# Expert layer of a two-layer trunk: two of eight experts go from 64 places to 32, and the turns are set anew

## The chip, the cores and the metric

The kernel runs on one core of a Trainium2 chip. The metric is the device time of one execution in microseconds (us); less is better. One execution was taken by the hardware profiler, and all rows below come from it.

## The reference

A residual trunk of two layers works on 256 tokens of width 1024 in float32. Each layer mixes the tokens (three groups side by side) and then applies a feed-forward part. In layer 0 that part is dense; in layer 1 it is a mixture of 8 experts, of which each token takes the two with the largest router logits. The change touches the experts alone:

```
def swiglu(h, wg, wu, wd):
    return (jax.nn.silu(h @ wg) * (h @ wu)) @ wd

logits = (t @ router).astype(jnp.float32)
top_v, top_i = lax.top_k(logits, TOP_K)             # 2 of 8
gates = jax.nn.softmax(top_v, axis=-1)
gate_full = jnp.sum(jax.nn.one_hot(top_i, 8) * gates[..., None], axis=1)
for e in range(8):
    out = out + gate_full[:, e:e + 1] * swiglu(t, wg[e], wu[e], wd[e])
```

An expert has 3584 inner columns, so its three matrices are 3 x 1024 x 3584 numbers, 44 MB in float32; all eight are 352 MB.

## The kernel before

The mixing of both layers and the dense part come first; the experts are the last part of the program (`experts`). Tokens are not multiplied by every expert. For each expert the kernel gathers the tokens that chose it into so many *places* (columns of a tile), by a product with a 0/1 matrix, and after the expert it scatters the result back by another such product.

**Order and kinds.** The eight experts are worked at places p = 0 to 7. Place 0 is always expert 0 (`FIXED`); the other seven experts are sorted by their count of tokens, most tokens first, so place 7 has the fewest. `KINDS` (L118) says how many places each has: places 1, 2, 3 are *wide*, 128 places (place 1 has 32 more, a second part of the kind `QUARTER`); places 0, 4, 5, 6, 7 are *narrow*, 64 places (`NARROW`). If an expert had more tokens than places, a flag is set, and code under it at the end (`rest`) runs that expert again for the tokens left over.

**Precision.** A wide block splits each weight tile into two fp32r parts (L196 on ScalarE, L197 on VectorE) and makes three products (L201 to L203). A narrow block multiplies the raw float32 weights: its 64 places take half of the array's columns, so two products run side by side on the column halves (L1467 up, L1534 down). A block in quarters has 32 places, and four run side by side (L1483 up, L1534 down).

**Blocks and loads.** An expert's 3584 inner columns are seven blocks of 512 (`NB`). A block's weights are six loads of 1 MiB: two for gate, two for up, two for down. Its up-part uses four of them and its down-part two. All loads go through one queue (SP) into 12 buffers, in the order in which the work uses them (`halves`); a load waits until the buffer 12 loads back is given free. A load is cut in two halves, which `take` hands out in order.

**Turns.** `work` (from L1541) runs 21 turns, one for each wide block, and one to end. Turn n does: transposes of the wide block before (`wide_T`, L1494, which are the mark of a turn's start below), the up-part of wide block n (with place 1 also its quarter, `quarter_up`), the down-part of the wide block before, the down-parts of the narrow blocks that were new in the turn before, and the up-parts of `TURNS[n]` new narrow blocks. Two narrow up-blocks (`LEAD`) come ahead of turn 0. The 35 narrow blocks come in the order of places 0, 4, 5, 6, 7, seven of each. So turns 0 to 6 carry two new narrow blocks each, and the 14 turns after them 1, 1, 2, 1, 1, 2, 1, 1, 2, 1, 1, 2, 2, 1.

**Around it.** `prepare` makes the gather of a place (L1249 for narrow places, L1263 for wide ones), some turns before the place is needed; it runs in steps between the products. `finish` scales an expert's result, splits it and scatters it (L1368 to L1381); at the last place it also stores the output. `small_T` transposes a narrow block's result for the down-part (L1506). The order of each engine's queue is set by the compiler's own scheduling of the written program.

Of the kernel before, what the change touches and what calls it, by code (L numbers as in the profile page):

```python
# [13 lines left out]
F32 = mybir.dt.float32  # L14
# [10 lines left out]
KD = DM // 128  # L25
# [89 lines left out]
WIDE, NARROW, QUARTER = "full", "half", "quarter"  # L115
PLACES = {WIDE: 128, NARROW: 64, QUARTER: 32}
IOTA = {WIDE: "iota", NARROW: "iota64", QUARTER: "iota32"}
KINDS = {0: (NARROW,), 1: (WIDE, QUARTER), 2: (WIDE,), 3: (WIDE,), 4: (NARROW,), 5: (NARROW,), 6: (NARROW,), 7: (NARROW,)}  # L118


WIDES = (1, 2, 3)
NARROWS = (0, 4, 5, 6, 7)

LEAD = 2
TURNS = [2] * 7 + [2 if _i % 3 == 2 or _i == 12 else 1 for _i in range(14)]
CAPS = [sum(PLACES[k] for k in KINDS[p]) for p in range(NE)]


@with_exitstack
def trunk(ctx: ExitStack, tc: tile.TileContext, x_in, pos_in, wst, moe, pp_in, rr_in, sw_in, rt_in,  # L130
# [969 lines left out]
    def experts():  # L1100
# [127 lines left out]
        def prepare(p, xg, sc):  # L1228

            kinds = KINDS[p]  # L1230
            n = sum(PLACES[kind] for kind in kinds)
            rs = []
            pe = big.tile([128, 2, 256], F32R, name="pe", tag="pe", bufs=1)
            for i, kind in enumerate(kinds):
                anchor[0] = one_hot(pe[:, :, i * 128:(i + 1) * 128], p, kind, 128 * i)
            for kind in kinds:
                if kind == WIDE:
                    xg.append((kind, big.tile([128, KD, 2, 128], F32R, name="xg", tag="xg", bufs=2), rs))
                else:
                    w = PLACES[kind]  # L1240
                    xg.append((kind, late.tile([128, KD, w], F32, name="xgs", tag="xgs" + kind, bufs=w // 32), rs))
            yield 1
            if kinds == (NARROW,):
                for k0 in range(0, KD, 4):
                    ps = pb()
                    for k in range(4):
                        ks = slice((k0 + k) * 128, (k0 + k + 1) * 128)
                        for i, (xc, t) in enumerate(((xh, 0), (xh, 1), (xl, 0), (xl, 1))):
                            T.matmul(ps[:, k * 64:k * 64 + 64], lhsT=xc[:, t, ks], rhs=pe[:, t, 0:64],  # L1249
                                     start=(i == 0), stop=(i == 3))  # L1250
                        if k == 1:
                            yield 1
                    act(xg[0][1][:, k0:k0 + 4], ps[:, 0:256].rearrange("p (k s) -> p k s", k=4), AF.Copy)
                    yield 1
            per = 512 // (2 * n) if kinds != (NARROW,) else KD + 1
            for k0 in range(0, KD if per <= KD else 0, per):
                ps = pb()
                p4 = ps[:, 0:per * 2 * n].rearrange("p (k c s) -> p k c s", k=per, c=2)
                for k in range(per):
                    ks = slice((k0 + k) * 128, (k0 + k + 1) * 128)  # L1260
                    for c, xc in enumerate((xh, xl)):
                        for t in range(2):
                            T.matmul(p4[:, k, c, :], lhsT=xc[:, t, ks], rhs=pe[:, t, 0:n], start=(t == 0), stop=(t == 1))  # L1263
                o = 0
                for kind, tile_, _ in xg:
                    w = PLACES[kind]
                    if kind == WIDE:
                        act(tile_[:, k0:k0 + per], p4[:, :, :, o:o + w], AF.Copy)
                    else:
                        d = tile_[:, k0:k0 + per]  # L1270
                        act(d, p4[:, :, 0, o:o + w], AF.Copy)
                        V.tensor_tensor(d, d, p4[:, :, 1, o:o + w], op=ALU.add)
                    o += w
                yield 1
            for i in range(len(kinds)):
                rs.append(rms_parts(pe, i * 128))
            for i in range(len(kinds)):
                scatter_parts(p, pe, i * 128, sc)
                yield 1
# [172 lines left out]
                    V.scalar_tensor_tensor(a, ps, rs[0], a, op0=ALU.mult, op1=ALU.mult)  # L1452
            return a, ws

        def narrow_up(st):

            _, z, rs = st
            a = ap_.tile([128, 256], F32, name="a", tag="a1", bufs=2)
            for j in range(2):
                ps = pb()[:, 0:256]  # L1460
                for q in range(4):
                    w = take()[2]
                    for kk in range(2):
                        k = q * 2 + kk
                        for hv in range(2):
                            o_ = kk * 512 + hv * 256
                            T.matmul(ps[HALF[hv], :], lhsT=z[:, k, :], rhs=w[:, o_:o_ + 256],  # L1467
                                     start=(k == 0), stop=(k == KD - 1))
                if j == 0:
                    act(a, ps, AF.Silu, scale=rs[0])  # L1470
                else:
                    V.scalar_tensor_tensor(a, ps, rs[0], a, op0=ALU.mult, op1=ALU.mult)  # L1472
            return a

        def quarter_up(st, ws):

            _, z, rs = st
            a = ap_.tile([128, 256], F32, name="a", tag="a2", bufs=1)
            ps = pb()[:, 0:256]
            for k in range(KD):  # L1480
                for g in range(4):
                    o_ = k % 2 * 512 + g % 2 * 256
                    T.matmul(ps[QUART[g], :], lhsT=z[:, k, :], rhs=ws[g // 2 * 4 + k // 2][:, o_:o_ + 256],  # L1483
                             start=(k == 0), stop=(k == KD - 1))
            act(a[HALF[1], :], ps[HALF[0], :], AF.Silu, scale=rs[1][HALF[0], :])
            V.scalar_tensor_tensor(a[HALF[1], :], ps[HALF[1], :], rs[1][HALF[1], :], a[HALF[1], :],
                                   op0=ALU.mult, op1=ALU.mult)
            return a

# [8 lines left out]
            V.tensor_tensor(z[:, :, 1, :], p3, z[:, :, 0, :].bitcast(F32), op=ALU.subtract)  # L1498
            return z

        def small_T(a, kind, rows=slice(None)):

            w = PLACES[kind]
            ps = pb()
            for j in range(2):
                T.transpose(ps[:, j * 2 * w:(j + 1) * 2 * w], a[rows, j * 128:(j + 1) * 128], ident[rows, rows])  # L1506
            z = ap_.tile([128, 4, w], F32, name="aT", tag="aT" + kind, bufs=64 // w % 2 + 1)
            act(z.rearrange("p (h j) s -> p j h s", h=2), ps[:, 0:4 * w].rearrange("p (j h s) -> p j h s", j=2, h=2),
                AF.Copy)
            return z  # L1510
# [29 lines left out]

        def work():  # L1541
            m, wjob = LEAD, None
            before = [(np_, ni, narrow_up(ready[np_][1][0])) for np_, ni in narrows[:LEAD]]
            drain()
            ask(NARROWS[1])
            for n in range(len(wides) + 1):

                if wjob is not None:
                    p, i, a, aq = wjob
                    aT = wide_T(a)  # L1550
                    aqT = small_T(aq, QUARTER, HALF[1]) if aq is not None else None
                prev, wjob = wjob, None
                if n < len(wides):
                    wp, wi = wides[n]
# [2 lines left out]
                    wjob = (wp, wi, a_, quarter_up(st[1], ws) if len(st) > 1 else None)  # L1557
                    if wi == 0 and wp != WIDES[-1]:
                        ask(WIDES[WIDES.index(wp) + 1])
                nT = [small_T(a_, NARROW) for _, _, a_ in before]  # L1560
                if prev is not None:
                    ws = wide_down(p, i, aT)
                    if i == NB - 1:
# [6 lines left out]
                            ended(p, QUARTER, [accs[p, QUARTER]])  # L1570

                for (np_, ni, _), z in zip(before, nT):
                    if ni == 0:
                        accs[np_] = [pa()]
                    small_down(accs[np_][0], NARROW, ni, z, [take()[2] for _ in range(4)])
                    if ni == NB - 1:
                        ended(np_, NARROW, accs[np_], np_ == NARROWS[-1])
                new = narrows[m:m + TURNS[n]] if n < len(wides) else []
                m += len(new)
                before = []  # L1580
                for np_, ni in new:
                    before.append((np_, ni, narrow_up(ready[np_][1][0])))
                    if ni == 0 and np_ != NARROWS[-1]:
                        ask(NARROWS[NARROWS.index(np_) + 1])

        def rest():

            any_ = nc.values_load(flag_i[0:1, 0:1], min_val=0, max_val=1)
            with tc.If(any_ > 0):
                for p in range(NE):  # L1590
                    o = CAPS[p]
                    for kind in (NARROW, WIDE):
                        if o >= SEQ:
                            break
                        here = nc.values_load(over_i[0:1, p:p + 1], min_val=0, max_val=SEQ)
                        with tc.If(here > o - CAPS[p]):
                            rest_of(p, kind, o)
                        o += PLACES[kind]
                    assert o >= SEQ
                for t in range(2):  # L1600
                    store(t, slice(0, DM))

        def rest_of(p, kind, o):
# [19 lines left out]
            for i in range(NB):  # L1623
# [13 lines left out]
                    else:  # L1637
                        V.scalar_tensor_tensor(a, ps, r, a, op0=ALU.mult, op1=ALU.mult)
                if kind == NARROW:
                    aT = small_T(a, NARROW)  # L1640
                else:
                    aT = ap_.tile([128, 4, 128], F32, name="af", tag="aT" + WIDE, bufs=1)
                    ps = pb()
# [178 lines left out]
```

## Time and profile before

| | us |
|---|---|
| median of 3 runs | 1455.73 |
| lowest and highest | 1454.22, 1458.97 |
| the profiled execution | 1454.79 |
| its span, first to last instruction | 1452.9 |
| PE busy in the span | 1390.3 |
| VectorE, ScalarE busy | 713.2, 630.8 |
| moved by DMA | 422.60 MB, of which 352.3 MB are the experts' weights |

Engines: PE is TensorE's matmul, PEld its weight load, DVE VectorE, ACT ScalarE, POOL GpSimd, SP the queue that issues loads. L1467 is line 1467 of the kernel. A group of rows is named by line, engine, operation and tile; "out<-in" are the program's names of tiles. Products are pipelined and their ends are modelled, so the mean of one product's record overlaps its neighbour; a run of products in the chain of waits gives the time they take together. Matmuls in float32 stand as two records each in the counts.

### The profile page before, as it was taken

The numbers are of one execution on the slowest core, as the hardware profiler recorded it, in microseconds if no ns is written. First come the engines' busy times: TensorE is split into PE (matmuls) and PEld (weight loads), VectorE is DVE, ScalarE is ACT, GpSimd is POOL, SyncE is SP. The second block draws the span as 40 slices with busy tenths as digits, with TensorE's granted clock in tenths as the row PEclk, the third lists the DMA queues.
The fourth block names the chain that finished last, engine by engine and source line by source line (L and its number), as shares of the span: only waits on it lengthen the run. The fifth ranks groups of instructions, "written<-read, shape, count | busy, mean of one in ns | idle before, by whom it ended". The sixth has DMA issues, their size and how long they took to land.

```text
span 1452.9 us, 23612 instructions
## 1 busy us (share of the span) xinstructions
PE 1390.3 (96%) x9620; PEld 1004.7 (69%) x9620; DVE 713.2 (49%) x1044; ACT 630.8 (43%) x986; POOL 76.6 (5%) x127
## 2 busy tenths in 40 slices
PE   7988899999998889999999999999999999999997
PEld 7977678888887767785666555666666666666663
DVE  5785454545658545243145224546355445454443
ACT  6657354444656723353134214434444434444341
POOL 1240000000125000000000000000000000000000
PEclk9999999999999897999999999999999999999998
DMA  7410255555441325699989998999999999999992
GB/s 277 173 60 2 88 174 186 192 174 184 152 173 59 103 116 213 243 399 426 403 363 375 420 378 366 426 391 414 372 426 427 383 427 427 426 426 426 426 427 115
DMA packets 59859, 422.60 MB, mean 291 GB/s; under 512 B 7136, under 2 KB 7136, under 8 KB 9824
## 3 DMA queue, kind: packets, MB, share of 16 engines
q1 hardware_dynamic: 59184, 420.03, 71.7%
q8 instruction: 77, 1.26, 0.3%
q10 hardware_dynamic: 560, 1.00, 0.2%
q14 instruction: 38, 0.31, 0.1%
HBM read 419.95 MB, written 1.05 MB: 290 GB/s over the span
## 4 chain that ended last, share of the span: by engine, by line
PE 84%; DVE 7%; ACT 3%; issue 2%; POOL 2%; DMA 1%; ACTq 0%; DVEq 0%; POOLq 0%
PE pb L1467 17%; PE pa L1534 10%; PE pb L202 8%; PE pb L203 8%; PE pb L201 7%; PE pa L202 6%; PE pa L201 6%; PE pa L203 6%; DVE wl L197 3%; PE pb L1483 2%; PE pb L1249 1%; PE pa L371 1%; PE pa L372 1%; PE pa L373 1%; POOL rq_y L209 1%
## 5 line engine op out<-in xcount | busy, mean ns | idle before, releaser
L197 DVE TENSOR_TENSOR wl<-raw,wh 128x1024 fp32r<-128x1024 f32 (+1 forms) x370 | 440.2, 1217 | 183.9 <-ACT wh L196 183.2
L196 ACT ACTIVATE wh<-raw 128x1024 fp32r<-128x1024 f32 (+1 forms) x370 | 380.8, 1053 | 226.8 <-PE pb L203 125.0
L1467 PE MATMUL pb<-raw,xgs 128*64 128x256 f32 x2240 | 254.2, 383 | 0.0
L1467 PEld LDWEIGHTS pb<-raw,xgs 128*64 128x64 f32 x2240 | 164.1, 138 | 88.3 <-issue 16.9
L202 PE MATMUL pb<-wl,xg 128*128 128x512 f32 x336 | 139.3, 415 | 14.6 <-DVE wl L197 13.7
L1470 ACT ACTIVATE a<-pb,rg 128x256 f32<-128x256 f32 x35 | 16.5, 473 | 304.9 <-PE pb L1467 304.9
L1534 PE MATMUL pa<-raw,aT 128*64 128x512 f32 (+1 forms) x784 | 143.1, 537 | 0.0
L201 PE MATMUL pb<-wh,xg 128*128 128x512 f32 x336 | 134.5, 403 | 0.0
L203 PE MATMUL pb<-wh,xg 128*128 128x512 f32 x336 | 132.5, 394 | 0.0
L1472 DVE SCALAR_TENSOR_TENSOR a<-pb,rg,a 128x256 f32<-128x256 f32 x35 | 16.9, 483 | 198.5 <-PE pb L1467 178.0
L1534 PEld LDWEIGHTS pa<-raw,aT 128*64 128x64 f32 (+1 forms) x784 | 45.0, 129 | 78.1 <-issue 67.0
L202 PEld LDWEIGHTS pb<-wl,xg 128*128 128x128 f32 x336 | 63.2, 188 | 44.5 <-DVE wl L197 27.8
L1498 DVE TENSOR_TENSOR aT<-pb,aT 128x512 fp32r<-128x512 f32 x21 | 14.5, 691 | 159.9 <-ACT aT L1497 159.9
L201 PEld LDWEIGHTS pb<-wh,xg 128*128 128x128 f32 x336 | 63.1, 188 | 20.8 <-ACT wh L196 6.9
L202 PE MATMUL pb<-wl,hTh 128*128 128x512 f32 (+1 forms) x192 | 73.0, 380 | 0.0
L203 PE MATMUL pb<-wh,hTl 128*128 128x512 f32 (+1 forms) x192 | 71.6, 376 | 0.0
L203 PEld LDWEIGHTS pb<-wh,xg 128*128 128x128 f32 x336 | 63.3, 188 | 11.9
L202 PE MATMUL pa<-wl,aT 128*128 128x512 f32 x168 | 68.4, 407 | 0.2 <-DVE wl L197 0.2
L201 PE MATMUL pb<-wh,hTh 128*128 128x512 f32 (+1 forms) x192 | 67.5, 378 | 0.8 <-ACT hTh L284 0.8
L203 PE MATMUL pa<-wh,aT 128*128 128x512 f32 x168 | 66.2, 394 | 0.0
L201 PE MATMUL pa<-wh,aT 128*128 128x512 f32 x168 | 57.6, 402 | 0.0
L201 PE MATMUL pa<-wh,hTh 128*128 128x512 f32 (+1 forms) x128 | 50.1, 406 | 3.9 <-ACT hTh L764 2.8
(384 smaller groups left out, 1987.0 us busy)
## 6 DMA issues: line engine op xcount, KB each, us to landing
raw<-moe SPq DMA_DIRECT2D x336, 1024.0 KB, 11.4
raw<-wst SPq DMA_DIRECT2D x54, 1024.0 KB, 4.9
raw<-wst SPq DMA_DIRECT2D x4, 832.0 KB, 5.3
area<-sw_in SPq DMA_DIRECT2D x2, 960.0 KB, 6.8
area<-sw_in SPq DMA_DIRECT2D x2, 664.0 KB, 6.4
x<-x_in SPq DMA_DIRECT2D x2, 512.0 KB, 5.2
raw<-wst SPq DMA_DIRECT2D x2, 512.0 KB, 7.4
out_dram<-x SPq DMA_DIRECT2D x4, 256.0 KB, 4.7
```

The costliest lines, as they stand in the source:

```text
L196: act(h[:, 0:n], t[:, a:b], AF.Copy)
L197: (E or V).tensor_tensor(lo[:, 0:n], t[:, a:b], h[:, 0:n].bitcast(F32), op=ALU.subtract)
L201: T.matmul(o, lhsT=xh, rhs=wh, start=first, stop=False)
L202: T.matmul(o, lhsT=xh, rhs=wl, start=False, stop=False)
L203: T.matmul(o, lhsT=xl, rhs=wh, start=False, stop=last)
L209: G.tensor_tensor(y, m, C("half")[:, 0:n], op=ALU.pow)
L371: T.matmul(ps, lhsT=wh[:, s_], rhs=hTh[:, k, :], start=(k == 0), stop=False)
L1467: T.matmul(ps[HALF[hv], :], lhsT=z[:, k, :], rhs=w[:, o_:o_ + 256], start=(k == 0), stop=(k == KD - 1))
L1470: act(a, ps, AF.Silu, scale=rs[0])
L1472: V.scalar_tensor_tensor(a, ps, rs[0], a, op0=ALU.mult, op1=ALU.mult)
L1483: T.matmul(ps[QUART[g], :], lhsT=z[:, k, :], rhs=ws[g // 2 * 4 + k // 2][:, o_:o_ + 256], start=(k == 0), stop=(k == KD - 1))
L1534: T.matmul(acc[rows, :], lhsT=aT[:, f, :], rhs=ws[f][:, g * w:g * w + w], start=(i == 0 and f == 0), stop=(i == NB - 1 and f == 3))
```

## The change

Place 0 and place 7 go from 64 places to 32. Their blocks are no longer multiplied on column halves but on column quarters, by the function that place 1's second part already used: `narrow_up` becomes `small_up`, which for such a place takes all eight halves of the up-part first and calls `quarter_up`; `small_down` runs with four column groups of 256 instead of two of 512, into a PSUM tile of 256 columns. The gather of these places writes 32 columns for each token group instead of 64. `finish` takes the form that place 1's second part had: one result of 256 columns, four row groups, eight adds of 256 columns, and at place 7 eight stores. None of the products is split in these blocks, as before. The number of loads and their bytes are the same. The code under the flag gets a third try for places that are smaller now.

The turns after the seventh carry 2, 1, 1, 2, 1, 2, 1, 1, 1, 2, 1, 1, 2, 1 new narrow blocks: ten instead of nine in turns 7 to 13, nine instead of ten in turns 14 to 20. The tile of a small block's result (tag `a1`) has three buffers instead of two, and place 1's second part uses them too.

```diff
-KINDS = {0: (NARROW,), 1: (WIDE, QUARTER), 2: (WIDE,), 3: (WIDE,), 4: (NARROW,), 5: (NARROW,), 6: (NARROW,), 7: (NARROW,)}
+KINDS = {0: (QUARTER,), 1: (WIDE, QUARTER), 2: (WIDE,), 3: (WIDE,), 4: (NARROW,), 5: (NARROW,), 6: (NARROW,), 7: (QUARTER,)}
...
-TURNS = [2] * 7 + [2 if _i % 3 == 2 or _i == 12 else 1 for _i in range(14)]
+TURNS = [2] * 7 + [2, 1, 1, 2, 1, 2, 1] + [1, 1, 2, 1, 1, 2, 1]
...
-                    w = PLACES[kind]
-                    xg.append((kind, late.tile([128, KD, w], F32, name="xgs", tag="xgs" + kind, bufs=w // 32), rs))
+                    m, w = (64, PLACES[kind]) if p in NARROWS else (32, 32)
+                    t = late.tile([128, KD, m], F32, name="xgs", tag=f"xgs{m}", bufs=m // 32)
+                    xg.append((kind, t[:, :, 0:w], rs))
             yield 1
-            if kinds == (NARROW,):
+            if p in NARROWS:
...
-                            T.matmul(ps[:, k * 64:k * 64 + 64], lhsT=xc[:, t, ks], rhs=pe[:, t, 0:64],
+                            T.matmul(ps[:, k * n:k * n + n], lhsT=xc[:, t, ks], rhs=pe[:, t, 0:n],
                                      start=(i == 0), stop=(i == 3))
...
-        def narrow_up(st):
-
-            _, z, rs = st
-            a = ap_.tile([128, 256], F32, name="a", tag="a1", bufs=2)
+        def small_up(p):
+            kind, z, rs = st = ready[p][1][0]
+            if kind == QUARTER:
+                return quarter_up(st, [take()[2] for _ in range(8)])
+
+            a = ap_.tile([128, 256], F32, name="a", tag="a1", bufs=3)
...
         def quarter_up(st, ws):
 
             _, z, rs = st
-            a = ap_.tile([128, 256], F32, name="a", tag="a2", bufs=1)
+            a = ap_.tile([128, 256], F32, name="a", tag="a1", bufs=3)
             ps = pb()[:, 0:256]
             for k in range(KD):
                 for g in range(4):
                     o_ = k % 2 * 512 + g % 2 * 256
                     T.matmul(ps[QUART[g], :], lhsT=z[:, k, :], rhs=ws[g // 2 * 4 + k // 2][:, o_:o_ + 256],
                              start=(k == 0), stop=(k == KD - 1))
-            act(a[HALF[1], :], ps[HALF[0], :], AF.Silu, scale=rs[1][HALF[0], :])
+            act(a[HALF[1], :], ps[HALF[0], :], AF.Silu, scale=rs[-1][HALF[0], :])
...
-            before = [(np_, ni, narrow_up(ready[np_][1][0])) for np_, ni in narrows[:LEAD]]
+            before = [(np_, ni, small_up(np_)) for np_, ni in narrows[:LEAD]]
...
-                nT = [small_T(a_, NARROW) for _, _, a_ in before]
+                nT = [small_T(a_, KINDS[np_][0], NARROW) for np_, _, a_ in before]
...
+                    kind = KINDS[np_][0]
                     if ni == 0:
-                        accs[np_] = [pa()]
-                    small_down(accs[np_][0], NARROW, ni, z, [take()[2] for _ in range(4)])
+                        accs[np_] = [pa()[:, 0:512 if kind == NARROW else 256]]
+                    small_down(accs[np_][0], kind, ni, z, [take()[2] for _ in range(4)])
...
-                    for kind in (NARROW, WIDE):
+                    for kind in (NARROW, WIDE, NARROW):
```

## Rows read from the trace of the kernel before

**Rows 1.** The page: granted clock and GB/s in 40 slices, then the loads.

```profile
PEclk9999999999999897999999999999999999999998
...
GB/s 277 173 60 2 88 174 186 192 174 184 152 173 59 103 116 213 243 399 426 403 363 375 420 378 366 426 391 414 372 426 427 383 427 427 426 426 426 426 427 115
...
raw<-moe SPq DMA_DIRECT2D x336, 1024.0 KB, 11.4
```

**Rows 2.** Busy time by stretch: stretch, length, engines, granted clock, DMA share, GB/s.

```profile
559.80:595.00 35.20, 35.20 (x237) 26.64 (x237) 14.89 (x47) 14.83 (x32) 0.00 (x0) 0.83 0.90 359
595.00:609.60 14.60, 14.60 (x135) 10.79 (x135) 3.52 (x9) 3.80 (x8) 0.00 (x0) 1.00 0.19 69
609.60:628.70 19.10, 19.10 (x147) 13.48 (x144) 5.11 (x5) 4.86 (x6) 0.00 (x0) 1.00 0.99 402
628.70:678.25 49.55, 49.55 (x378) 33.13 (x378) 17.50 (x23) 18.45 (x25) 0.00 (x0) 1.00 0.98 406
678.25:723.05 44.80, 44.80 (x323) 28.62 (x324) 12.93 (x14) 11.89 (x16) 0.00 (x0) 1.00 1.01 408
723.05:920.40 197.35, 194.45 (x1399) 119.35 (x1400) 72.02 (x80) 64.75 (x85) 0.00 (x0) 1.00 0.93 384
920.40:1178.40 258.00, 253.94 (x1477) 169.33 (x1477) 125.47 (x147) 106.39 (x133) 0.00 (x0) 1.00 0.97 406
1178.40:1426.70 248.30, 240.62 (x1378) 157.01 (x1378) 118.67 (x119) 102.85 (x122) 0.00 (x0) 1.00 1.00 421
1426.70:1452.90 26.20, 16.80 (x74) 8.92 (x70) 12.65 (x17) 6.53 (x9) 0.00 (x0) 0.86 0.12 43
```

**Rows 3.** The same view, one long stretch inside the last third.

```profile
1140.00:1420.00 280.00, 271.57 (x1542) 177.19 (x1540) 135.07 (x139) 117.30 (x139) 0.00 (x0) 1.00 1.01 426
```

**Rows 4.** Waits of PE from 560 us on: total us, times, longest.

```profile
PE pb L202 <- DVE wl L197: 13.7, 17, 1.3
PE pb L1506 <- DVE a L1472: 0.6, 1, 0.6
```

**Rows 5.** Chain of waits in order of time: start us, us, what.

```profile
603.65 3.59 PE pb L1483 x64
...
611.20 6.92 PE pa L1534 x32
...
664.44 13.81 PE pb L1467 x128
...
702.03 8.88 PE pa L1534 x64
...
723.05 0.59 PE pb L1494 x4
...
726.21 1.71 PE pb L1249 x16
...
1178.43 0.59 PE pb L1494 x4
...
1437.51 1.87 PE pa L1534 x8
```

**Rows 6.** Groups by line from 620 us on: busy us, mean ns, idle before.

```profile
L1381 DVE TENSOR_TENSOR x<-x,pb 128x512 f32<-128x512 f32 x32 | 20.8, 679 | 2.6 <-PE pb L1380 2.6
...
L1470 ACT ACTIVATE a<-pb,rg 128x256 f32<-128x256 f32 x32 | 15.1, 473 | 286.4 <-PE pb L1467 286.4
...
L1381 DVE TENSOR_TENSOR x<-x,pb 128x256 f32<-128x256 f32 x8 | 3.1, 417 | 1.2 <-PE pb L1380 1.1
...
L1485 ACT ACTIVATE a<-pb,rg 64x256 f32<-64x256 f32 x6 | 2.8, 467 | 9.9 <-PE pb L1483 9.9
```

**Rows 7.** Busy time in 10 us of turn 3, expert 1's quarter among it.

```profile
740.00:750.00 10.00, 10.00 (x83) 6.46 (x83) 4.55 (x5) 3.35 (x5) 0.00 (x0) 1.00 0.57 204
```

**Rows 8.** Busy time and granted clock before and as the experts start.

```profile
550.00:560.00 10.00, 6.97 (x39) 6.78 (x38) 6.68 (x31) 4.12 (x12) 3.45 (x4) 0.56 0.00 1
560.00:570.00 10.00, 10.00 (x44) 7.41 (x45) 6.10 (x21) 5.65 (x8) 0.00 (x0) 0.50 0.93 358
570.00:580.00 10.00, 10.00 (x88) 6.36 (x86) 1.84 (x4) 1.35 (x3) 0.00 (x0) 0.92 0.95 365
```

More of the change, by code (lines that the diff above doesn't have):

```diff
@@ L1252, in prepare @@
                             yield 1
-                    act(xg[0][1][:, k0:k0 + 4], ps[:, 0:256].rearrange("p (k s) -> p k s", k=4), AF.Copy)
+                    act(xg[0][1][:, k0:k0 + 4], ps[:, 0:4 * n].rearrange("p (k s) -> p k s", k=4), AF.Copy)
                     yield 1
-            per = 512 // (2 * n) if kinds != (NARROW,) else KD + 1
-            for k0 in range(0, KD if per <= KD else 0, per):
+            per = 512 // (2 * n)
+            for k0 in range(0, 0 if p in NARROWS else KD, per):
                 ps = pb()
@@ L1484, in quarter_up @@
                              start=(k == 0), stop=(k == KD - 1))
-            act(a[HALF[1], :], ps[HALF[0], :], AF.Silu, scale=rs[1][HALF[0], :])
-            V.scalar_tensor_tensor(a[HALF[1], :], ps[HALF[1], :], rs[1][HALF[1], :], a[HALF[1], :],
+            act(a[HALF[1], :], ps[HALF[0], :], AF.Silu, scale=rs[-1][HALF[0], :])
+            V.scalar_tensor_tensor(a[HALF[1], :], ps[HALF[1], :], rs[-1][HALF[1], :], a[HALF[1], :],
                                    op0=ALU.mult, op1=ALU.mult)
@@ L1499, in wide_T, with small_T @@
             return z
-        def small_T(a, kind, rows=slice(None)):
+        def small_T(a, kind, tag):
             w = PLACES[kind]
+            rows = HALF[1] if kind == QUARTER else slice(None)
             ps = pb()
@@ L1506, in small_T @@
                 T.transpose(ps[:, j * 2 * w:(j + 1) * 2 * w], a[rows, j * 128:(j + 1) * 128], ident[rows, rows])
-            z = ap_.tile([128, 4, w], F32, name="aT", tag="aT" + kind, bufs=64 // w % 2 + 1)
+            z = ap_.tile([128, 4, 64 if tag == NARROW else w], F32, name="aT", tag="aT" + tag,
+                         bufs=2 if tag == NARROW else 1)[:, :, 0:w]
             act(z.rearrange("p (h j) s -> p j h s", h=2), ps[:, 0:4 * w].rearrange("p (j h s) -> p j h s", j=2, h=2),
@@ L1550, in work @@
                     aT = wide_T(a)
-                    aqT = small_T(aq, QUARTER, HALF[1]) if aq is not None else None
+                    aqT = small_T(aq, QUARTER, QUARTER) if aq is not None else None
                 prev, wjob = wjob, None
@@ L1572, in work @@
                 for (np_, ni, _), z in zip(before, nT):
+                    kind = KINDS[np_][0]
                     if ni == 0:
-                        accs[np_] = [pa()]
-                    small_down(accs[np_][0], NARROW, ni, z, [take()[2] for _ in range(4)])
+                        accs[np_] = [pa()[:, 0:512 if kind == NARROW else 256]]
+                    small_down(accs[np_][0], kind, ni, z, [take()[2] for _ in range(4)])
                     if ni == NB - 1:
-                        ended(np_, NARROW, accs[np_], np_ == NARROWS[-1])
+                        ended(np_, kind, accs[np_], np_ == NARROWS[-1])
                 new = narrows[m:m + TURNS[n]] if n < len(wides) else []
@@ L1581, in work @@
                 for np_, ni in new:
-                    before.append((np_, ni, narrow_up(ready[np_][1][0])))
+                    before.append((np_, ni, small_up(np_)))
                     if ni == 0 and np_ != NARROWS[-1]:
@@ L1639, in rest_of @@
                 if kind == NARROW:
-                    aT = small_T(a, NARROW)
+                    aT = small_T(a, NARROW, NARROW)
                 else:
```

## The prediction, made from the kernel before and the diff

> **What bounds the kernel now.** Read the page first [rows 1]. From the 18th of the 40 slices to the 39th, all of it expert layer, the granted clock stands at nine tenths or more and the transfers between 363 and 427 GB/s, at 420 or over in 12 of the 22. 336 loads of 1 MiB are its weights. Then the stretches between turns [rows 2]: PE is busy almost all the time, and the transfers run at 384 to 408 GB/s up to 1178 us and at 421 after it. Whether that is the transfers' own limit shows in 280 us inside the last third [rows 3]: 426 GB/s with the queue never idle, that is 1.0486 MB / 426 = 2.46 us a load, and 336 loads take 827 us. So two limits lie on top of each other. The waits of PE's own say which of them ends last [rows 4]: 13.7 us behind the splits on VectorE in 17 short waits, the rest under 1 us, and none behind a load. Up to turn 13 PE is the limit and the loads have gaps, because all 12 buffers are full; in the last third both are at theirs at once.
>
> **The price of one block.** In the chain of waits [rows 5] two narrow up-blocks of 64 places take 13.81 us, 6.90 each; the same up-block in column quarters (64 instructions of expert 1's second part) takes 3.59. That is 3.31 less. Two narrow down-blocks take 6.92, 3.46 each; one quarter and two narrow take 8.88, so a quarter takes 1.96: 1.50 less. Together 4.81 us a block, and 14 blocks (seven of place 0, seven of place 7) give PE back 67 us. The gathers give nothing: 32 matmuls stay 32, and 16 of them take 1.71 us at 64 columns. ScalarE's silu takes 467 ns on 64 rows against 473 on 128 [rows 6]; ScalarE and VectorE gain nothing either, and keep their splits. No load is saved, so 67 us is not what the time can fall by.
>
> **The head, up to turn 3.** I count loads, which the code fixes: 8 for the two leading blocks, 16 in turn 0, 18 in each of turns 1 and 2, so 60 before the mark at 723.05 (the transposes that open turn 3) [rows 5]. The loads have a hole: 69 GB/s from 595 to 609.6 [rows 2]. There the 21st load waits for a buffer that expert 1's quarter product at 603.65 gives back [rows 5]. Both leading up-blocks lie ahead of that product, so the hole shrinks by 2 x 3.31 = 6.6 us. Bytes of the stretches after 723.05 without the final stores (384 x 197.35 + 406 x 258 + 421 x 248.3 = 285.1 MB) are 271.9 loads, so 64.1 had moved by the mark: the 60th landed 4.1 x 2.46 = 10.2 us ahead of it, at 712.8. Moved by the hole it lands at 706.2; where the small gaps in the three stretches after the hole (19.1, 49.55 and 44.8 us at 402, 406 and 408 GB/s, 5.3 us lost against 426) close as well, at 700.9. PE alone would be there sooner: seven ups and six downs are 23.2 + 9.0 = 32.2 us, 690.9. So the loads set the mark. I take the middle, 703.5: 19.5 us gained, and some 12 us of PE's saving are lost as waiting.
>
> **The middle, turns 3 to 13.** One quarter down-product is left (1.5 less); everything else in turns 3 to 6 stays. The new turns put ten narrow blocks of 64 places into turns 7 to 13 where nine stood: 6.90 + 3.46 = 10.4 more. PE needs the 455 us it needed before plus 9; the loads for it, 176, need 433. PE stays the limit. The mark that opens turn 14 moves from 1178.4 to 1178.4 - 19.5 - 1.5 + 10.4 = 1167.8.
>
> **The last third.** By that mark the changed kernel has used 236 loads (230 before). Before, 99.7 loads moved after it (421 x 248.3 / 1.0486) [rows 2], so 236.3 had moved: 6.3 ahead, with full buffers. With the same lead 93.7 loads are left, 230.5 us: the last one lands at 1398.3. PE alone needs from the mark to its last product, 1439.4 [rows 5], 261.0 before; minus one block moved away (10.4) and seven quarter blocks (33.7) 216.9, which is 1384.7. So here the loads set the end, with 13.6 us to spare for PE, and the extra block in the middle costs nothing net: with the old turns the mark would be at 1157.4 but 99.7 loads would follow, to 1402.7. After the last landing come half a quarter down-product (1.0) and the ending: before 13.5 us from the last product to the end of the span. Its adds become eight of 417 ns for four of 679 [rows 6], 0.6 more, and the stores eight for four; the ending of expert 3 moves into the waiting. I take 0.5 in all, between -2.7 (that ending's four adds off the path) and +3 (four more stores in turn). 1398.3 + 1.0 + 13.5 + 0.5 = 1413.3 of span; 1.9 lie around the span of the profiled execution (1454.79 against 1452.9), so 1415.2 against 1454.79. The median of the runs is 0.9 above that execution: **1416**.
>
> Bounds of this sum: the lead in loads 4.1 (as at 723) to 7, so +5.4 to -1.7; the head -2.6 to +2.7; the ending -3.2 to +2.5; a turn of two narrow blocks more in the middle has its own wait at its start, up to 1.3 [rows 4]. That is 1408 to 1428. Without any gap after the hole the loads would end at 603.0 + 315 x 2.46 = 1378, the time 1396: no better is possible.
>
> The rows show 426 GB/s held for 280 us [rows 3]. The Trainium skill, "DMA: Bandwidth & Descriptors", section "Where 436 GB/s comes from", has the memory side bind at about 358 GB/s a core for loads from HBM. By it a load would take 2.93 us, the loads would be the limit everywhere already, and the change would give nothing; the trace disagrees with 426 over 358.
>
> **Rivals.** *Held buffers, slower.* A quarter block takes all four loads before its first product and reads gate and up side by side, so it holds four of twelve buffers to its end. Expert 1's quarter holds them too, behind a wide block, and there the loads fall to 204 GB/s in a 10 us stretch [rows 7]: 5.2 us lost. If each of the 12 quarter blocks after the two leading ones cost the loads as much, 62 us would come on top: 1478, slower. It decides from 3.3 us a block on (12 x 3.3 is the whole gain). Against it: the hold is 3.6 us instead of a wide block and a quarter, and the loss at 740 falls where PE was behind with full buffers.
>
> *Queues.* Eight takes ahead of the products put the next wide block's first splits ahead of the quarter's silu on ScalarE and its multiply on VectorE, which run in order; these splits wait for loads not yet landed, and PE's four PSUM tiles behind them. It bites where loads are the limit, at most one load (2.46) for each of five head blocks: 12 us, 1428. For it: the new order of the queues is unseen. Against: in the last third PE has 13.6 us to spare.
>
> *The clock.* After PE had waited in the routing, the granted clock was 0.50 from 560 to 570 and back within the next 10 us [rows 8], 1.2 GHz instead of 2.4; since then it was full. The changed kernel waits for loads in turns 0 to 2 and 14 to 20. If it fell once in each of the seven late turns for 10 us, PE would lose 5 us a turn, 35 in all, 21 more than its 13.6 to spare; half of them would cost 4, and head turns have some 12 us of waiting to give. I take +12: 1428. The Trainium skill, "TensorE: Matmul & The Clock Gate", section "HAM oscillation — how this bites in real kernels", describes this: waits for loads between short bursts of products slow the clock each time. Rows 8 agree that waiting lowers it; none here shows it inside the expert layer.
>
> *It doesn't do what it says.* If place 0 or 7 had more than 32 tokens, the code under the flag would run another 42 loads, 103 us: about 1520. The reference's routing, worked out on its inputs, gives expert 0 16 tokens and the emptiest expert 14.
>
> **How the numbers follow.** Forecast 0.70, queues 0.10, clock 0.06, held buffers 0.06, too many tokens 0.01; 0.05 that gains and losses cancel for a reason I don't see, 0.02 slower by such a one. About 0.3% is what a measurement of this kernel can tell from no change. Faster: 0.70 + 0.10 + 0.06 = 0.86; same 0.05; slower 0.09. The forecast's own range, 1408 to 1428, holds most of its 0.70; with the two rivals at 1428 and a few us for what lies beside them, 1402 to 1433 holds 8 in 10.
>
> **What would show it.** In the profile after: up-blocks on the quarter line of 3.6 us; the mark of turn 3 at 701 to 706, that of turn 14 near 1168; in the last third 426 GB/s up to a last landing near 1398 and PE waiting for loads there, its last product ending 1 to 2 us after that landing, where before it ended at 1439.4 and the loads near 1426.7 (what the last stretch of rows 2 still moves, 1.1 MB, is the stores). Wrong would be: gaps between loads in turns 0 to 2 or 14 to 20 (held buffers), ScalarE's silu long after its product (queues), a clock below 1.00 in the last third, or a mark of turn 14 over 1175.

## The result, and the profile after

| | before | after |
|---|---|---|
| median, us | 1454.97 (4 runs) | 1416.35 (4 runs) |
| lowest and highest | 1452.42, 1458.97 | 1414.25, 1419.55 |
| span of the profiled execution | 1452.9 | 1412.5 |
| first up-block of the experts starts | 565.0 | 562.55 |
| mark of turn 3 | 723.05 | 698.15 |
| mark of turn 14 | 1178.43 | 1161.6 |
| last load has landed | 1426.7 | 1395.2 |
| last product of a down-block ends | 1439.4 | 1398.1 |

The ratio is 0.973, with an interval of 0.970 to 0.976: 2.7% faster. The part ahead of the experts is the same code in both, and differs by 2.45 us in these two executions; over all profiles of this study it ends between 560.9 and 570.2. So stages below are compared from that start where it matters.

Three lines of the pages: the chain of waits that ended last, by engine, before and then after, and the rate after in 40 slices (of 35.3 us), to be set beside [rows 1].

```profile
PE 84%; DVE 7%; ACT 3%; issue 2%; POOL 2%; DMA 1%; ACTq 0%; DVEq 0%; POOLq 0%
...
PE 76%; DMA 10%; DVE 6%; ACT 3%; POOL 2%; issue 2%; SPq 0%; ACTq 0%; DVEq 0%; POOLq 0%
...
GB/s 285 178 61 2 90 153 185 189 188 179 159 185 74 84 159 71 337 425 425 425 427 425 426 385 374 426 372 426 402 426 413 420 427 426 426 411 426 427 426 226
```

In the chain of before PE had 84% and the transfers (DMA) 1%; now a tenth of the chain runs through loads. Busy time by stretch, cut at the same marks as [rows 2]:

```profile
592.00:603.90 11.90, 11.90 (x204) 7.03 (x202) 1.24 (x2) 1.18 (x4) 0.00 (x0) 1.00 0.70 268
603.90:648.00 44.10, 40.87 (x410) 28.95 (x408) 18.19 (x23) 17.86 (x26) 0.00 (x0) 0.96 1.01 426
648.00:698.10 50.10, 46.13 (x417) 27.18 (x415) 17.66 (x18) 16.05 (x22) 0.00 (x0) 0.97 1.01 426
698.10:894.00 195.90, 192.55 (x1425) 119.91 (x1423) 72.87 (x84) 64.73 (x85) 0.00 (x0) 1.00 0.98 409
894.00:1161.50 267.50, 264.28 (x1560) 174.81 (x1558) 125.74 (x148) 107.91 (x135) 0.00 (x0) 1.00 0.99 413
1161.50:1395.20 233.70, 212.14 (x1434) 139.83 (x1436) 124.39 (x124) 105.78 (x125) 0.00 (x0) 0.98 1.00 420
1395.20:1412.50 17.30, 8.47 (x60) 5.09 (x52) 6.93 (x15) 1.75 (x3) 0.00 (x0) 0.80 0.20 65
```

The stretch that was the hole in the loads (69 GB/s before) moves 268 GB/s, and the two stretches after it run at 426, the loads' own pace, with PE idle for 3 to 4 us in each. In the last stretch before the final landing PE is busy for 212 of 234 us. PE's waits from the experts on show the same: the second and third line are waits for a load, the third by way of ScalarE's copy of it. [Rows 4] had neither.

```profile
PE pb L202 <- DVE wl L197: 12.4, 16, 1.3
PE pb L1486 <- DMA raw<-moe: 10.1, 10, 3.7
PE pb L201 <- ACT wh L196: 9.9, 6, 1.7
```

From the chain of waits: a quarter up-block, the two marks, three loads one behind the other at the end, and pieces of what follows them.

```profile
630.56 3.59 PE pb L1486 x64
...
698.15 0.59 PE pb L1497 x4
...
1161.61 0.58 PE pb L1497 x4
...
1328.82 19.50 DMA raw<-moe
...
1348.33 19.61 DMA raw<-moe
...
1368.05 19.51 DMA raw<-moe
...
1387.64 1.06 ACT wh L196
...
1388.73 1.24 DVE wl L197
...
1397.06 1.00 PE pa L1539 x16
```

The chain of the last 60 us before 1387.6 is loads alone, each 19.5 us from issue to landing: eight stand in the queue, and one lands every 2.45 us.

### The profile page after: what moved, and what is told of

Read it like the earlier page. It is cut to its first block, busy times and chain, and to the rows that moved or that the text cites. A ratio compares the mean times of both kernels' runs of the same rounds, so it can differ in the third digit from the quotient of the medians.

```text
span 1412.5 us, 24089 instructions
## 1 busy us (share of the span) xinstructions
PE 1330.2 (94%) x9860; PEld 965.4 (68%) x9860; DVE 715.0 (51%) x1052; ACT 629.0 (45%) x986; POOL 77.9 (6%) x127
## 4 chain that ended last, share of the span: by engine, by line
PE 76%; DMA 10%; DVE 6%; ACT 3%; POOL 2%; issue 2%; SPq 0%; ACTq 0%; DVEq 0%; POOLq 0%
PE pb L1470 10%; DMA raw<-moe 10%; PE pb L202 8%; PE pb L201 7%; PE pb L203 7%; PE pa L1539 7%; PE pa L202 6%; PE pa L201 6%; PE pa L203 6%; PE pb L1486 4%; DVE wl L197 2%; PE pb L1250 1%; PE pa L371 1%; PE pa L373 1%; PE pa L372 1%
## 5 line engine op out<-in xcount | busy, mean ns | idle before, releaser
L1470 PE MATMUL pb<-raw,xgs 128*64 128x256 f32 x1344 | 151.0, 380 | 0.0
L201 PE MATMUL pb<-wh,xg 128*128 128x512 f32 x336 | 136.7, 409 | 9.9 <-ACT wh L196 9.9
L203 PE MATMUL pb<-wh,xg 128*128 128x512 f32 x336 | 134.0, 399 | 0.0
L1470 PEld LDWEIGHTS pb<-raw,xgs 128*64 128x64 f32 x1344 | 95.0, 137 | 54.7 <-issue 9.3
L1539 PE MATMUL pa<-raw,aT 128*32 128x256 f32 (+1 forms) x1008 | 120.1, 454 | 0.0
L1486 PE MATMUL pb<-raw,xgs 128*32 128x256 f32 x1344 | 93.1, 395 | 10.1 <-DMA raw<-moe 10.1
L1473 ACT ACTIVATE a<-pb,rg 128x256 f32<-128x256 f32 x21 | 9.9, 473 | 174.9 <-PE pb L1470 174.9
L1539 PEld LDWEIGHTS pa<-raw,aT 128*32 128x32 f32 (+1 forms) x1008 | 42.8, 118 | 61.9 <-issue 46.2
L1486 PEld LDWEIGHTS pb<-raw,xgs 128*32 128x32 f32 x1344 | 45.2, 113 | 50.9 <-DMA raw<-moe 14.1
L203 PE MATMUL pa<-wh,aT 128*128 128x512 f32 x168 | 66.5, 396 | 0.0
L1475 DVE SCALAR_TENSOR_TENSOR a<-pb,rg,a 128x256 f32<-128x256 f32 x21 | 10.2, 484 | 99.4 <-PE pb L1470 99.4
```

Source lines behind the costliest of these rows:

```text
L201: T.matmul(o, lhsT=xh, rhs=wh, start=first, stop=False)
L203: T.matmul(o, lhsT=xl, rhs=wh, start=False, stop=last)
L1539: T.matmul(acc[rows, :], lhsT=aT[:, f, :], rhs=ws[f][:, g * w:g * w + w], start=(i == 0 and f == 0), stop=(i == NB - 1 and f == 3))
```

## The experiments

All are made from the changed kernel. In the table "start" is the first up-block in the profiled execution, and the other times are counted from it. Each ratio is taken against executions of before from the same batch (medians 1455.6 in this table, 1455.81 in the runs below it, 1454.97 for the change), so it is not quite the quotient of the medians shown.

| kernel | median, us | ratio to before | start | mark 3 | mark 14 | last product | end of span |
|---|---|---|---|---|---|---|---|
| before | 1454.97 | 1 | 565.0 | 158.1 | 613.4 | 874.4 | 887.9 |
| turns only | 1454.38 | 0.9985 (0.9962 to 1.0009) | 563.6 | 158.0 | 623.4 | 874.0 | 888.3 |
| place 7 only, old turns | 1446.76 | 0.9933 (0.9907 to 0.9959) | 564.4 | 158.0 | 613.4 | 865.6 | 880.7 |
| place 0 only, old turns | 1433.75 | 0.984 (0.979 to 0.989) | 570.2 | 135.3 | 589.7 | 850.4 | 864.2 |
| both, old turns | 1421.94 | 0.976 (0.971 to 0.980) | 566.6 | 135.4 | 589.1 | 839.7 | 854.4 |
| the change | 1416.35 | 0.973 (0.970 to 0.976) | 562.55 | 135.6 | 599.1 | 835.5 | 850.0 |

**Place 0 alone.** Place 7 at 64 places, old turns:

```diff
-KINDS = {0: (QUARTER,), ... 7: (QUARTER,)}
+KINDS = {0: (QUARTER,), ... 7: (NARROW,)}
-TURNS = [2] * 7 + [2, 1, 1, 2, 1, 2, 1] + [1, 1, 2, 1, 1, 2, 1]
+TURNS = [2] * 7 + [2 if _i % 3 == 2 or _i == 12 else 1 for _i in range(14)]
```

> The changed kernel, with place 7 back at 64 places and the old turns: only place 0 has 32. Theory (loads set the head, PE the middle, and in the last third both stand at their limits): the mark of turn 3 comes as early as in the changed kernel, the middle takes what it took before, and the last third takes PE's old 261 us. So 21 to 22 us less than before, 1433. Rival (PE's saving counts wherever it falls): 7 x 4.81 = 33.7 less, 1421. Rival (held buffers cost the loads): less than 10 us gained.

Measured 1433.75. The mark of turn 3 comes 22.8 us earlier, and from there to the last product the kernel takes 715.1 us, where before took 716.3: the gain is made in the head and carried, unchanged, to the end. In turns 1 and 2 the loads run at their pace; in the last third loads and PE are both busy nearly all the time, as before:

```profile
612.90:705.50 92.60, 85.17 (x825) 54.11 (x823) 35.60 (x41) 33.60 (x47) 0.00 (x0) 0.98 1.01 426
1159.90:1407.60 247.70, 240.09 (x1374) 156.79 (x1372) 118.51 (x119) 103.01 (x121) 0.00 (x0) 1.00 1.00 423
```

Seven blocks at 4.81 us would be 33.7; about a third of that doesn't reach the time. In turns 1 and 2 alone PE is now idle for 7.4 us (92.6 - 85.2), where before it had no idle time [rows 2].

**Place 7 alone.** The other way round (`0: (NARROW,)`, `7: (QUARTER,)`, old turns).

> The changed kernel, with place 0 back at 64 places and the old turns: only place 7 has 32. Theory: head and middle as before, mark of turn 14 at 1178; the last landing stays where it was, near 1425, for the loads were at their limit there, and only PE's 13 us behind it go. 1442. Rival (PE's saving counts wherever it falls): 33.7 less, 1421. Rival (clock): the granted clock falls below 0.95 in the last third and the time stays above 1450.

Measured 1446.76: of 33.7 us of PE's saving 8 reach the time, 5 fewer than forecast. Both marks and the last landing (861.4 us after the start, 861.6 before) are where they were, so the loads do set the last third. What was missed lies behind the landing: the last product ends 4.2 us after it and not 1, and the ending takes 15.1 us. Busy time of the last third, then of the stretch around the last landing and of the ending:

```profile
1177.70:1425.80 248.10, 225.65 (x1505) 148.35 (x1504) 125.28 (x125) 106.54 (x127) 0.00 (x0) 0.95 1.00 422
...
1413.00:1430.00 17.00, 14.05 (x119) 8.38 (x119) 6.61 (x8) 6.12 (x9) 0.00 (x0) 0.90 0.60 253
1430.00:1445.00 15.00, 5.98 (x24) 4.17 (x24) 6.29 (x15) 0.47 (x1) 0.00 (x0) 0.65 0.24 75
```

Three products of the last wide down-part, one behind the other in PE's timeline:

```profile
1421.37 0.63 PE L203 MATMUL pa<-wh,aT 128*128 128x512 f32 x1
1421.80 0.63 PE L202 MATMUL pa<-wl,aT 128*128 128x512 f32 x1
1422.23 0.63 PE L203 MATMUL pa<-wh,aT 128*128 128x512 f32 x1
```

The granted clock is 0.95 in the last third: with PE waiting for loads it falls to its lower level, 1.2 GHz, now and then, as the clock's rival had it. Inside the third that costs nothing, for the last load lands when it did. One such fall came as the last wide down-part ran, 1421.0 to 1424.4, just ahead of the last landing (1425.8), and PE was busy from there to its last product: the products follow each other at 0.43 us, against 0.23 at the full clock. Seven products at 0.2 more are 1.4 us of the 5. Another 1.9 is the split of the last wide loads and the products behind it, which the changed kernel has too (below). The landing itself is 0.8 later than forecast, and the ending is 1.1 longer; 0.4 of that is in the changed kernel as well, and the cause of the other 0.7, which lies behind the last add, stays open.

**Both, old turns**, and **the turns alone**:

> The changed kernel with the old turns. Theory: the mark of turn 14 comes 10 us earlier than in the changed kernel (near 1151), but 99.7 instead of 93.7 loads follow it, so the last landing comes 4 us later, near 1399: 1420. The parts add up to more than single ones here only by what PE and loads give each other: 21 + 13 = 34 less than before, no 67. Rival (the new turns carry the gain): over 1430.

> The changed kernel with places 0 and 7 back at 64: only the new turns are left. Theory: PE is the limit to the end, and its work is the same, so the mark of turn 14 comes 10 us later (1189) and the end where it was: 1455, within 3 us. Rival (the turns smooth the loads and are a gain by themselves): 4 us less or more.

Measured 1421.94 and 1454.38, both near the theory. The turns alone put the mark of turn 14 10.0 us later and the end nowhere. On top of both quarter places they do the same to that mark (589.1 to 599.1), yet the last product comes 4.2 us earlier: six fewer loads follow the mark. In the medians that is 5.6 us, but the intervals of the two overlap, so for the time the turns' share is not shown. The traces, one of each kernel, do bear it out: counted from the start, pairs that should agree (before and the turns alone, the change and the interleaved loads below) have their last products within 0.4 us of each other.

**Half the bytes for place 7.** Do the loads really set the last third?

```diff
+                if half:
+                    nc.sync.dma_start(t[:, 0:1024], src[:, 0:1024])
...
+                    if p == 7:
+                        a_, b_ = 0, 1024
```

> The changed kernel, but each load of place 7 fetches half its columns (0.5 MiB) and both halves of the products read these, so place 7's result isn't the expert's; PE's work is the same. Theory (loads set the last third): 42 loads are half as long, 52 us less for the queue, and PE sets the end of the last third again, 14 us earlier by the forecast's sum: 1402, between 1396 and 1406. Rival (PE with its waits, the queues of ScalarE and VectorE or the clock set the last third, the loads only look full): within 3 us of the changed kernel, 1416.

Measured 1405.45, a ratio of 0.965 (0.962 to 0.968): 11 us faster than the changed kernel with the same work on PE. Busy time from the mark of turn 14 (1163.5) to the last product:

```profile
1163.50:1389.00 225.50, 213.62 (x1464) 141.02 (x1463) 125.25 (x126) 106.77 (x127) 0.00 (x0) 0.98 0.86 338
```

The queue has air (338 GB/s), the last load lands 18 us before the last product, and PE needs 225.2 us from the mark; the forecast's sum had 216.9 for it. So the loads did set this third, and PE had some 8.5 us to spare there (233.7 - 225.2), less than the 13.6 of the sum. The 8 us can be split. From the mark to the last product PE was busy for 252.5 us before and is for 213.3 now, 39.2 less where 44.1 were counted; of the 4.9 that are missing some 3 are an estimate for 6.9 us at the lower clock (1318.7 to 1322.2 and 1380.2 to 1383.6). And it is idle for 11.9 us instead of 8.5: waits for ScalarE's copy of a load (5.0 us, none before) are new:

```profile
PE pb L201 <- ACT wh L196: 5.0, 3, 1.7
PE pb L202 <- DVE wl L197: 4.9, 5, 1.3
```

**All small places at 32.** The rival of the held buffers, pushed as far as it goes: 35 quarter blocks.

```diff
-... 4: (NARROW,), 5: (NARROW,), 6: (NARROW,), 7: (QUARTER,)}
+... 4: (QUARTER,), 5: (QUARTER,), 6: (QUARTER,), 7: (QUARTER,)}
-    put("caps", np.array(CAPS)[None, :])
+    put("caps", float(SEQ))
```

> The changed kernel with 32 places for places 4, 5 and 6 too, and the flag never set: tokens of these experts beyond 32 are left out. All 35 small blocks are quarter blocks. Theory: PE is no limit anywhere after the head, so the loads run without gaps from the end of the hole (near 600) on, 315 x 2.46 us: 1396. Rival (held buffers: a quarter block holds four of twelve buffers to its end and makes gaps): with 35 of them instead of 14 the gaps grow, GB/s below 420 in every third, 1410 or more.

Measured 1404.47. The rate by thirds:

```profile
607.00:944.00 337.00, 307.64 (x2767) 194.58 (x2765) 144.88 (x169) 125.97 (x168) 0.00 (x0) 0.95 1.01 425
944.00:1163.50 219.50, 196.14 (x1474) 135.22 (x1473) 110.67 (x129) 93.07 (x116) 0.00 (x0) 0.95 1.01 426
1163.50:1384.50 221.00, 188.69 (x1356) 122.98 (x1358) 108.83 (x112) 91.03 (x108) 0.00 (x0) 0.94 0.99 418
```

PE's two longest waits:

```profile
PE pb L1486 <- DMA raw<-moe: 40.9, 31, 3.7
PE pb L201 <- ACT wh L196: 32.2, 20, 2.7
```

The time lies between the theory's 1396 and the rival's 1410, but the loads have no gaps to speak of. Of the 11 loads behind the 60th that land 0.4 to 1.0 us late, nine have eight loads in the queue, so no held buffer keeps them back: a quarter block that holds its four buffers costs the loads next to nothing, and that rival falls. The time is still 8 us over the expected floor. The hole ends where it was counted (the 21st load lands at 602.9), but the last one lands at 1384.5 and not 1378: 2.48 us a load on the mean, not 2.46. And 19.1 us follow that landing, where 15 were counted. The floor of this kernel, with these loads, is nearer 1404 than 1396.

**Loads of a quarter block interleaved.**

```diff
+        UPS = {NARROW: (0, 1, 2, 3), QUARTER: (0, 2, 1, 3)}
...
+                if lazy and k % 4 == 0:
+                    for j in (0, 1, 4, 5):
+                        ws[j + k // 2] = take()[2]
```

> The changed kernel; a quarter block's four up-loads come in the order gate, up, gate, up instead of gate, gate, up, up, and its products take four halves, run four of the eight steps, and take the other four: fewer loads held, fewer splits put ahead of its silu. Theory: the loads set these stretches, so nothing changes: 1416, within 4 us. Rivals (held buffers, queues): 5 us or more faster.

Measured 1415.47, 0.973 (0.969 to 0.976), so no difference beyond the few us that the intervals leave: neither held buffers nor the splits ahead of the silu cost the changed kernel anything that can be measured. The splits do get ahead of it, but seldom. In the changed kernel ScalarE's silu starts within 0.1 us of its product in 19 of 21 quarter blocks, and 2.6 us after it in two (products that end at 654.4 and 1387.1). Here the second delay is gone, and the last product comes 835.7 us after the start, against 835.5. The second one in the changed kernel, the products and the silu behind two splits:

```profile
1385.16 1.92 PE L1486 MATMUL pb<-raw,xgs 128*32 128x256 f32 x28 [0.53 <-DMA raw<-moe]
...
1389.68 0.47 ACT L1488 ACTIVATE a<-pb,rg 64x256 f32<-64x256 f32 x1
```

**Another order, other turns.** If the turns of expert 1 are where PE is behind, place 7's quarter blocks belong there:

```diff
-NARROWS = (0, 4, 5, 6, 7)
+NARROWS = (0, 7, 4, 5, 6)
-TURNS = [2] * 7 + [2, 1, 1, 2, 1, 2, 1] + [1, 1, 2, 1, 1, 2, 1]
+TURNS = [1, 2, 1, 2, 2, 1, 2] + [1, 2, 1, 2, 2, 2, 1] + [1, 1, 2, 2, 1, 2, 2]
```

> The changed kernel with place 7's blocks right after place 0's (order 0, 7, 4, 5, 6) and other turns: 11 new small blocks in turns 0 to 6, 11 in turns 7 to 13, 11 in turns 14 to 20. Quarter blocks then meet the turns with expert 1's quarter, where PE is behind the loads, and blocks of 64 places the later turns. Theory: PE is behind nowhere for long, the loads run at 420 GB/s or more from the hole to the end: 1396 to 1402. Rival (the middle's PE limit only moves on): 1412 or more.

Measured 1404.44, 0.966 (0.961 to 0.970): 12 us faster than the change, faster than both kernels, and as fast as the kernel with all small places at 32, though no token is left out. By thirds, cut at the marks of turns 1, 8 and 14 and at the last landing:

```profile
606.00:872.00 266.00, 255.18 (x2292) 164.69 (x2288) 121.64 (x136) 108.97 (x144) 0.00 (x0) 0.99 1.00 420
872.00:1115.90 243.90, 239.65 (x1470) 156.61 (x1468) 109.91 (x133) 91.52 (x115) 0.00 (x0) 1.00 1.01 426
1115.90:1385.40 269.50, 261.48 (x1504) 168.84 (x1502) 126.35 (x132) 109.67 (x132) 0.00 (x0) 1.00 1.00 421
```

The loads run at 420 to 426 GB/s from the hole to the end, and PE is busy for 96 to 98% of each third. This bears the forecast's middle out: in the change, 409 and 413 GB/s there were PE's limit, and with PE's saving moved there they are gone. The time is 2.4 us over the range expected for this kernel: its last load lands at 1385.4, as with 32 places everywhere, and 17 us follow. Order and turns were changed together, so what each of them gives is not shown.

## Why the prediction was right, point by point

The forecast was 1416, and 1416.35 came. The steps, in the profiled execution (the sum had a span of 1413.3; it was 1412.5). Its signs in the profile came only roughly: turn 3's mark 3 us ahead of its window, turn 14's 6 us ahead, 420 GB/s in the last third instead of 426, and a clock of 0.98 there, which it had named as a sign of being wrong.

- *Price of a block.* 3.59 us for the up-block, as forecast. 67 us were to come back to PE; its busy time fell by 60.1 (1390.3 to 1330.2). Some 7 to 8 us went to the lower clock (an estimate, see the clock below), which makes up the 67.
- *Head.* The mark of turn 3 was to lie at 703.5 and came at 698.15: 2.45 us of it are the earlier start, 2.9 the sum. The hole lost 12.2 us of loading before and loses 4.4 now, 7.8 less where 6.6 were counted, and the small gaps after it closed altogether, where I had taken half. Place 0 alone, with the same mark, shows that this part is its doing.
- *Middle.* 464.3 us from mark to mark in the sum, 463.45 measured. The extra block cost its 10.4 (10.0 with the turns alone), and PE stayed the limit at 409 and 413 GB/s.
- *Last third.* 93.7 loads were to follow the mark; 420 x 233.7 / 1.0486 gives 93.6. They took 233.6 us, not 230.5: 420 GB/s, not 426. Five of them land 0.5 to 0.8 us late, 3.4 us in all, with three to five loads in the queue; why they do isn't shown. Half the bytes for place 7 showed that the loads and not PE set this third; PE's 13.6 us to spare in the sum were 8.5.
- *Ending.* 1.0 + 13.5 + 0.5 us were counted after the last landing, and 17.3 came. The mis-sized term is the first: the last product follows the landing by 2.9 us, because the two wide loads landed shortly before it still pass ScalarE's copy, VectorE's subtraction and 24 wide products, four of which run after the landing (the chain shows the first two at 1387.64 and 1388.73, 2.3 us together). The sum took only the quarter's half product. The rest is the ending itself, 14.4 instead of 14.0.

So five terms were off by -2.45, -2.9, -0.85, +3.1 and +2.3 us, -0.8 together: the mechanism was right, and that its sizes cancelled to less than a microsecond is luck, the first of them being the start of that one execution. The number is better than the working.

Of the rivals, *queues* and *held buffers* fell with the interleaved loads and with 35 quarter blocks at 425 GB/s. *The clock* did fall where PE waits: 0.96 and 0.97 in turns 1 and 2, 0.98 in the last third. These are the four stretches at the lower level in the experts of the changed kernel, and a quarter up-block in the third of them, behind PE's longest wait: 60 of its 64 records take 6.54 us, where all took 3.59.

```profile
613.60:617.00 3.40, 3.40 (x12) 2.82 (x12) 3.00 (x3) 2.80 (x5) 0.00 (x0) 0.50 1.00 424
657.90:661.40 3.50, 3.50 (x10) 2.74 (x9) 3.44 (x5) 2.60 (x3) 0.00 (x0) 0.51 1.02 428
1347.40:1354.30 6.90, 5.94 (x56) 2.76 (x58) 0.00 (x0) 0.00 (x0) 0.00 (x0) 0.51 1.00 419
1357.70:1361.10 3.40, 3.29 (x8) 2.61 (x9) 3.40 (x4) 2.39 (x3) 0.00 (x0) 0.50 1.03 434
...
1348.36 6.54 PE L1486 MATMUL pb<-raw,xgs 128*32 128x256 f32 x60 [3.68 <-DMA raw<-moe]
```

PE was busy for 16.1 us of them; with products at 0.43 us instead of 0.23 (place 7 alone) that is some 7 to 8 us of its time, an estimate. The Trainium skill describes such falls behind waits for loads in "TensorE: Matmul & The Clock Gate", section "HAM oscillation — how this bites in real kernels". The trace agrees with the fall, but the time doesn't follow: in all four stretches the loads run on at 419 to 434 GB/s, and with the clock at 0.94 to 0.95 through all three thirds of the kernel with 32 places everywhere, they still ran at 418 to 426 GB/s and set its time. It costs where loads don't hold PE up any more: 1.4 us just ahead of the last landing with place 7 alone, and some 3 us, by estimate, with half the bytes for place 7, where PE sets the last third. The code under the flag did not run: 336 loads, as before.

What each part is worth, from the spans counted from the start: place 0 23.7 us, place 7 by itself 7.2, both 33.5, with the new turns 37.9. The 67 us of PE's saving are nearly twice what the time shows. From the start to the end PE's busy time fell by 58.1 us (863.9 to 805.8) and its idle time grew by 20.1, nearly all of it the waits for loads and for ScalarE's copies of them shown above; that leaves 38.

## What to carry to other kernels

Where an engine and the loads are both near their limits, ask stage by stage which of them is ahead and by how many buffers; a saving on the engine counts only up to the next point at which it meets the loads, and a part that gains little by itself (place 7: 7 us) may gain more where the engine is behind. A saving is best moved to the stage that needs it: the same quarter blocks, put into the turns where PE was behind, with other turns after them, were worth another 12 us. Add the pieces after the last landing one by one, splits included, for there nothing hides them.

## What the runs showed of the hardware

The granted clock went to its lower level and back again and again in a kernel that was never idle for more than a few us in its experts (a mean of 0.946 over the span with 32 places everywhere, PE's longest wait 3.7 us), and nothing of it could be seen in that kernel's rate of loads. One core took 425 to 426 GB/s from its memory for 280 us on end in the kernel before [rows 3] and for 556 us (607 to 1163.5) with 32 places everywhere. Pauses of 0.4 to 1.0 us come in between, most of them with eight loads in the queue; over the 315 loads behind the hole they make 2.48 us a load out of the 2.46 of the best stretches.
